# Queries ordered behind products, two fetches on GpSimd, and a third place for the parts of probabilities

## The chip, the core and the metric

The kernel runs on one core of one Trainium2 chip. A core has a matrix engine (TensorE, PE in the profile; PEld is its loading of stationary operands), three engines for elementwise work (VectorE or DVE, ScalarE or ACT, GpSimd or POOL) and a fifth, SyncE (SP), which here only issues transfers. Transfers (DMA) are carried by 16 engines that all issuers share; SP, ACT and POOL each have a queue of their own. Every engine works through its own list of instructions in order and waits, at the head of that list, for semaphores of the others. The metric is the time of one execution on the device in microseconds; several are taken and the median is given.

## The reference

The program is one step of a small hybrid model with two layers, on 256 prompt tokens and 1,024 latent tokens of 1,024 channels, ten tiles of 128 tokens in all.

```python
for l in range(DEPTH):                        # DEPTH = 2
    sh, sc, gt = split_mod(silu(c) @ w_ada[l] + b_ada[l])
    h = rms_norm(x, norm_g[l]) * (1 + sc) + sh
    if l % 2 == 0:                            # gated linear attention, forward and backward scans
        out, state = gla_mixer(h, ...)        # (rms_norm(o_f + o_b) * silu(gate)) @ w_out
    else:                                     # grouped-query softmax attention
        q, k, v, gate = split(h @ w_in)       # 8 query heads, 2 key heads, 128 wide
        q, k = rms_norm(q, qn), rms_norm(k, kn)      # latent tokens: rope_2d as well
        p = softmax(q @ k.T * HEAD_DIM ** -0.5)      # latent: 1024 keys + 256 cached ones
        out = ((p @ v) * silu(gate)) @ w_out
    x = x + gt * out
```

Prompt tokens attend to the 256 prompt keys only. Returned are both groups of tokens, the scan states and the prompt's keys and values.

## The kernel before

To keep the precision of float32, every matrix operand is scaled by a power of two and split into two float16 parts, high and low, and each product is three matmuls: high by high, high by low, low by high (`mm3`, line 124). So most steps have the same form: an engine makes the high part, DVE the low part, and a DMA transpose, issued by SP, turns them so that the contracted index lies on the partitions.

The work has four stages. The first, to about 585 us, is the linear attention: a loop of 50 slots (`gla`, four heads and one more, ten token tiles each), into which a function `filler(slot)` puts other work: weights of later stages, and for the first four latent row tiles the fetch of the branch rows `og_d` with their scaling, splitting and transposing (`out_load`, line 827, and `out_prep`, line 835). The tuple `PREP` names the slots in which this happens, `EARLY` the slots in which the first two of these rows already go through the output product.

The second stage, to about 736 us, is `gla_out` (line 849). It goes over the eight row tiles left, in the order latent, then prompt (`n` is the place in that order, from 2 to 9). At each place it forms the residual tile: the output product `y` on PE, 24 matmuls of 512 columns and 48 of 256, the scaled sum with the input row `xr` (`residual`, lines 810 to 822), the norm and modulation for the next layer (`mod_tile`), and two transposes into `hT_hi` and `hT_lo` (line 377). Between residual tiles it puts key tiles (`key_tile`, 48 matmuls of 256 columns into `kv`, line 1041) and, at the end, the first query tiles (`query`, line 1193, whose matmuls go to `mm`). The branch rows of places 4 and later are fetched here, by `out_load` (line 832), into the two halves of a buffer `og` which lies where the scan's `q` and `k` buffers were; `out_prep` finds their maximum (line 838), makes the high part on ACT (841), the low part on DVE (842), and issues the two transposes on SP (844 and 845). In places 4 and 5 the text calls the tile "row 4" and "row 5".

The third stage, to about 1205 us, is `attention` (line 1205): ten steps `n`, each a pair of a head group and a block of 256 tokens, four heads `e` in each, two query tiles `j` of 128 in each head. For each: the scores `S` on PE (line 1104), the maximum on DVE (1107), the exponential `p` on ACT (1112), then in `rest` (line 1118) the reciprocal of the sum, and the two parts of the probabilities in one buffer `phl`: the high part by POOL where `j` is 0 (1134) and by ACT where it is 1 (1136), the low part by DVE (1137); SP transposes the whole buffer into `PT` (1138), and two heads later PE multiplies `PT` by the values (`values`, line 1151). `phl` has two buffers, used in turn. The keys, values and gates of the prompt and the last key tiles come in the first heads of this stage.

The fourth stage, `att_out`, forms the output product. Its first branch row, 1 MB from `og2_d`, is fetched within the third (`out2_load`, line 1257) into a buffer of the pool `wst`, of which one was given to the transposed queries and the other is free in attention until then. Below, `wst` also names the transposed queries and keys in a row of the profile.

The order of each engine's list is not the order of the Python statements. A planner replays the program with modelled costs and lets each engine take the instruction that it holds to be ready first; `issue_after(x)` keeps all instructions made under it behind instruction `x`. So a matmul whose operands the planner expects early may stand ahead of one that was written before it. Buffers count as well: an instruction may only write a place whose earlier readers are through.

Of the kernel before, what the change touches and what calls it, by code (L numbers as in the profile page):

```python
# [7 lines left out]
F16 = mybir.dt.float16  # L8
BF16 = mybir.dt.bfloat16
F32 = mybir.dt.float32  # L10
# [7 lines left out]
P = 128  # L18
D = 1024
KT = D // P  # L20
TP, TS = 256, 1024
# [3 lines left out]
PAST = 256  # L25
# [11 lines left out]

WO = (30, 32, 36, 38)

PREP = (42, 44, 46, 48)  # L40
EARLY = (45, 47)

AHEAD = (3, 5, 7, 9, 13, 15, 17, 19, 21, 23, 25, 27, 29, 31)
# [10 lines left out]
class K:  # L54
# [69 lines left out]
    def mm3(self, out, lhs, rhs, n=KT):  # L124
        for k in range(n):
            lh, ll = lhs(k)
            rh, rl = rhs(k)
            for j, (a, b) in enumerate(((lh, rh), (lh, rl), (ll, rh))):
                self.nc.tensor.matmul(out, a, b, start=k == 0 and j == 0, stop=k == n - 1 and j == 2)  # L129

    def hT(self, k, a, n):
        return self.hT_hi[:, k, a : a + n], self.hT_lo[:, k, a : a + n]
# [691 lines left out]

    def out_load(self, i, og=None, parts=None):
        if og is None:
            og = self.og[:, i % 2]
            t = self.t(self.xp, [P, 2 * D], F16, "oghl", bufs=2)  # L830
            parts = t[:, 0:D], t[:, D:]
        self.nc.sync.dma_start(og, self.og_d[i])
        return i, og, parts

    def out_prep(self, i, og, parts):
# [13 lines left out]
    def gla_out(self, wo, early, n0):  # L849
        nc = self.nc  # L850
        order = [2, 3, 4, 5, 6, 7, 8, 9, 0, 1]
        prep = dict(zip(order, early))
        self.inv_h = self.mod1[3]
        self.og = self.t(self.xp, [P, 2, D], F32, "og")
        half = self.t(self.xp, [P, 2, KT, 256], F16, "wkv")
        xs, rows = {}, {}

        def load(n):
            if n < NT:
                xs[n] = self.t(self.xp, [P, D], F32, "xr", bufs=4)  # L860
                (nc.gpsimd if n < n0 + 2 else nc.sync).dma_start(xs[n], xrow(self.I, order[n]))

        load(n0)
        load(n0 + 1)
        for n in range(len(early), n0 + 4):
            rows[n] = self.out_load(order[n])
        ckv = self.att_load()
        for n in range(n0, NT):
            i = order[n]
            if n == NT - 1:  # L870
                self.query_rest()
                self.query()
                self.key_tile(order[n - 2], wkv)
                self.query_rest()
            hT, lT, inv = prep.pop(i)
            x = xs.pop(n)
            last = self.residual(i, lambda k: (hT[:, k, :], lT[:, k, :]), wo, inv, x)
            nc.gpsimd.dma_start(self.x1_d[i], x)
            self.last = last
            with self.tc.issue_after(last):  # L880
                if n + 2 in rows:
                    prep[order[n + 2]] = self.out_prep(*rows.pop(n + 2))
            load(n + 2)
            if n + 4 in range(len(early), NT):
                rows[n + 4] = self.out_load(order[n + 4])
            t = self.t(self.xp, [P, 2, D], F16, "hl", bufs=2)
            if i == 0:
                self.rows_load(0)
            self.mod_tile(i, x, (t[:, 0], t[:, 1]), self.last)
            for j in {3: (0,), 4: (1, 2), 5: (3,), 6: (4,), 7: (5,), 8: (6,)}.get(n, ()):  # L890
                self.key_tile(order[j], wkv)
            if n == 8:
                self.query()
            if n == n0:
                d, inv = self.ahead["kv"]
                wkv = []
                for j, (hi, lo) in enumerate((
                    [t[:, :, 256:512] for t in self.nw[0:2]], (half[:, 0], half[:, 1])
                )):
                    b = slice(256 * j, 256 * j + 256)  # L900
                    nc.sync.dma_start(hi, d[:, 0, :, b])
                    nc.sync.dma_start(lo, d[:, 1, :, b])
                    wkv.append((hi, lo, 256))
                with self.tc.issue_after(last):
                    self.att_setup(*ckv)
                    self.key_setup(*ckv, inv)
            if n == 4:
                self.q0 = self.t(self.wp, [P, KT, 512], F16, "whi2")
                nc.sync.dma_start(self.q0, self.ahead["q0"][0][:, 0])
            if n == 7:  # L910
                self.query_start()
        self.query_low()
        return wkv[0]
# [204 lines left out]
    def rest(self, after=None):  # L1118
        if self.put_off is None:
            return  # L1120
        if after is not None:
            with self.tc.issue_after(after):
                return self.rest()
        nc = self.nc
        p, den, PT, j, nk = self.put_off
        self.put_off = None
        r = self.t(self.sm, [P, 1], F32, "srec")
        nc.vector.reciprocal(r, den)  # L1128
        r2 = self.t(self.sm, [P, 1], F32, "srec2")
        nc.vector.tensor_scalar(r2, r, 2.0 ** 14, None, ALU.mult)  # L1130
        parts = self.t(self.sp, [P, 2 * (TS + PAST)], F16, "phl")[:, 0 : 2 * nk]
        hi, lo = parts[:, 0:nk], parts[:, nk:]
        if j == 0:
            nc.gpsimd.tensor_scalar(hi, p, r, 2.0 ** 14, ALU.mult, ALU.mult)  # L1134
        else:
            nc.scalar.activation(hi, p, AF.Copy, scale=r2)  # L1136
        nc.vector.scalar_tensor_tensor(lo, p, r2, hi, ALU.mult, ALU.subtract)  # L1137
        nc.sync.dma_start_transpose(PT[:, 0 : 2 * nk // P, j * P : j * P + P], parts)  # L1138
# [66 lines left out]
    def attention(self, wo, wk):  # L1205
        self.S0, self.put_off = self.t(self.ps, [P, 1536], F32, "S"), None
        wq, wg, q, g = self.wq, self.wg, self.q, {}
        pend, later = [], []
        t = self.t(self.sp, [P, 20, 256], F16, "PT", bufs=3)[:, 0:16, :].rearrange("p (j k) n -> p j k n", j=2)
        for j in range(2):  # L1210
            self.nc.sync.dma_start(t[:, j], self.ahead["kv"][0][:, j, :, 256:512])
        wkv = [wk, (t[:, 0], t[:, 1], 256)]
        for n, (p, c) in enumerate(self.steps):
            if n == 1:
                wq.append(self.load_w("q1", 1, later))
            if n == 4:
                wg.append(self.load_w("g1", (2, 0), later))
            if n == 6:
                wo.append(self.wload("o0", (0, 2), later))
            if n == 9:  # L1220
                wo.append(self.wload("o1", 1, later))
            for e in range(4):
                h = 4 * p + e
                if later:
                    self.nc.sync.dma_start(*later.pop(0))
                PT = self.t(self.sp, [P, 20, 256], F16, "PT", bufs=3)
                self.scores(h, c, 0, q[(p, c, 0)], PT)
                if e % 2 == 0:
                    self.query()
                    self.rest()  # L1230
                    self.scores(h, c, 1, q[(p, c, 1)], PT)
                else:
                    self.query_rest()
                if len(pend) == 2:
                    self.values(*pend[0], g.pop(pend.pop(0)[0]))
                else:
                    self.key_tile(len(pend), wkv)
                if e % 2 == 1:
                    self.scores(h, c, 1, q[(p, c, 1)], PT)
                pend.append((h, c, PT))  # L1240
                if e % 2 == 1:
                    g.update({i: self.gateT(i, c, *wg[p]) for i in (h - 1, h)})
                    self.rest()
                if n == 9 and e == 0:
                    row = self.out2_load(OUT[0])
                if n == 9 and e == 1:
                    first = self.ropet.rearrange("p a b d -> p (a b d)").bitcast(F16)
                    first = first.rearrange("p (j h t) -> p j h t", j=2, h=AH)
                    with self.tc.issue_after(self.last):
                        self.prep = self.out2_prep(row, (first[:, 0], first[:, 1]))  # L1250
        self.fold_gate(*self.gate_load(1), wo[0][2] + wo[1][2])
        wo[:] = [(hi, lo, 512) for hi, lo, _ in wo]
        self.out_tile(OUT[0], 0, self.t(self.sp, [P, TS + PAST], F32, "p")[:, 0:D], wo)
        for t in pend:
            self.values(*t, g.pop(t[0]))
# [50 lines left out]
def emit(ctx, tc, I, O, dbg=None, stop=None):  # L1306
# [29 lines left out]
    with ExitStack() as c:  # L1336
# [102 lines left out]
        def filler(slot):  # L1439
# [32 lines left out]
            if slot == 40:  # L1472
# [7 lines left out]
                k.rows_load(1)  # L1480
            if slot in PREP:
                n = PREP.index(slot)
                a = k.t(k.wst, [P, KT, 256], F32, "wst").rearrange("p k n -> p (k n)")[:, 0:D]
# [138 lines left out]
```

## Time and profile before

| | |
|---|---|
| median of 3 runs (lowest to highest) | 1309.43 us (1306.7 to 1311.03) |
| the profiled execution | 1308.64 us |
| its span, first to last instruction | 1306.6 us |
| busy in the span: PE, DVE, ACT, POOL | 93%, 71%, 54%, 28% |
| mean busy share of the 16 transfer engines, `gla_out` and attention to 1130 us | 0.79 and 0.71 |

All times in rows of the profile count from the start of the span. A row of the list of groups or of the timeline names the line of the kernel, the engine, the operation, the written and the read tile, the shape and how many instructions it merges; a bracket at the end of a timeline row gives the idle time of the engine before it and what ended it. `SPq` is SP's queue: its durations are the times that the issuing took. A row of the list of waits reads: engine, tile and line that waited, for whom, microseconds in total, how often, the longest one. Buffer numbers are left out, so `mm` stands for query products, gates and values alike.

### The profile page before, as it was taken

What the parts mean: (1) busy time and instruction counts of PE and PEld (TensorE: products, weight loads), DVE (VectorE), ACT (ScalarE), POOL (GpSimd) and SP (SyncE); (2) the same over time, 40 slices, a digit from 0 to 9 for tenths busy, and PEclk for the clock granted to TensorE, in tenths of its full rate; (3) what the DMA queues carried; (4) which work ended last, traced back from release to release, by engine and by line L of the source; (5) the groups of instructions that cost most, each with busy time, mean ns of one, the idle gap of its engine ahead of it and who ended that gap; (6) DMA issues with size and microseconds to landing.
All of it is one profiled execution on the core that took longest, in us unless ns stands there. A gap on an engine that the chain in (4) does not pass through costs nothing. (4 is left out here: it accounts for less than half of the span.)

```text
span 1306.6 us, 22246 instructions
## 1 busy us (share of the span) xinstructions
PE 1215.6 (93%) x7936; PEld 783.7 (60%) x7936; DVE 924.6 (71%) x2120; ACT 705.4 (54%) x1706; POOL 360.7 (28%) x594
## 2 busy tenths in 40 slices
PE   3899999999998989796999989999998999989998
PEld 2366666555645556574777557667665767766444
DVE  5575879877876798676776767777767587785652
ACT  3684656565655566541333376766766686673110
POOL 1132214223321143410223334342232345322000
PEclk9899999999998999998999999999999999999999
DMA  9712655554646343269956597666957648879342
GB/s 359 251 33 82 211 158 175 172 162 135 187 135 193 118 145 114 88 159 284 240 129 170 146 209 142 129 138 131 199 108 157 142 95 146 185 140 227 128 150 81
DMA packets 357454, 207.51 MB, mean 159 GB/s; under 512 B 251054, under 2 KB 341438, under 8 KB 354912
## 3 DMA queue, kind: packets, MB, share of 16 engines
q1 hardware_dynamic: 349824, 188.02, 56.2%
q0 software_dynamic: 4080, 12.73, 3.2%
q10 hardware_dynamic: 3440, 5.35, 1.1%
q8 instruction: 62, 1.02, 0.3%
q14 instruction: 48, 0.39, 0.1%
HBM read 107.45 MB, written 37.26 MB: 111 GB/s over the span
## 5 line engine op out<-in xcount | busy, mean ns | idle before, releaser
L129 PEld LDWEIGHTS <-hT_hi 128*128 128x128 f16 x1920 | 188.6, 98 | 133.4 <-issue 18.4
L129 PE MATMUL mm<-whi,hT_hi 128*128 128x512 f16 (+1 forms) x576 | 200.4, 348 | 13.7 <-DMA whi<-w_q 8.9
L129 PE MATMUL mm<-whi,hT_lo 128*128 128x512 f16 (+1 forms) x576 | 200.1, 347 | 0.1
L129 PE MATMUL mm<-wlo,hT_hi 128*128 128x512 f16 (+1 forms) x560 | 194.2, 347 | 0.0
L129 PEld LDWEIGHTS <-whi 128*128 128x128 f16 x1232 | 121.1, 98 | 61.3 <-issue 2.5
L1137 DVE SCALAR_TENSOR_TENSOR phl<-p,srec,phl 128x1280 f16<-128x1280 f32 (+1 forms) x80 | 108.7, 1360 | 68.5 <-POOL phl L1134 35.7
L129 PE MATMUL mm<-hT_hi,whi 128*128 128x256 f16 (+1 forms) x480 | 142.1, 296 | 0.0
L129 PE MATMUL mm<-hT_lo,whi 128*128 128x256 f16 (+1 forms) x480 | 142.0, 296 | 0.0
L129 PE MATMUL mm<-hT_hi,wlo 128*128 128x256 f16 (+1 forms) x480 | 141.9, 296 | 0.0
L129 PEld LDWEIGHTS <-hT_lo 128*128 128x128 f16 x960 | 94.5, 98 | 65.7 <-DMA hT_lo<-k 3.4
L1104 PE MATMUL S<-kT,wst 128*128 128x512 f16 (+1 forms) x624 | 122.0, 338 | 9.9 <-ACT p L1112 8.7
L129 PE MATMUL mm<-PT,vh 128*128 128x256 f16 x672 | 114.0, 275 | 11.8 <-DMA PT<-phl 8.7
L1107 DVE TENSOR_REDUCE smx<-S 128x1 f32<-128x1280 f32 (+1 forms) x80 | 101.6, 1269 | 14.3 <-PE S L1104 14.2
L1134 POOL TENSOR_SCALAR phl<-p,srec 128x1280 f16<-128x1280 f32 (+1 forms) x40 | 56.0, 1401 | 192.6 <-DVE srec L1128 77.7
L1112 ACT ACTIVATE p<-S,snb,sexp 128x1280 f32<-128x1280 f32 (+1 forms) x80 | 99.4, 1242 | 5.6 <-DVE phl L1137 1.8
L1104 PEld LDWEIGHTS <-wst 128*128 128x128 f16 x624 | 60.9, 98 | 62.3 <-issue 10.3
L129 PE MATMUL mm<-PT,vl 128*128 128x256 f16 x336 | 92.6, 276 | 0.0
L152 DVE TENSOR_REDUCE wmx<-wst 128x1 f32<-128x512 f32 x104 | 64.8, 677 | 21.2 <-DMA wst<-in_att_w_in 7.8
L129 PEld LDWEIGHTS <-vh 128*128 128x128 f16 x672 | 65.7, 99 | 23.3 <-issue 9.6
L129 PEld LDWEIGHTS <-wlo 128*128 128x128 f16 x616 | 60.6, 98 | 31.7 <-DVE wlo L1275 1.8
L942 POOL TENSOR_TENSOR rope<-hx,ropet 128x64 f32<-128x64 f32 x160 | 63.2, 425 | 30.7 <-ACT hx L1068 18.2
L1109 ACT ACTIVATE snb<-smx,nsexp 128x1 f32<-128x1 f32 x80 | 23.3, 291 | 74.9 <-DVE smx L1107 72.9
(370 smaller groups left out, 2710.2 us busy)
## 6 DMA issues: line engine op xcount, KB each, us to landing
wada<-in_w_ada SPq DMA_DIRECT2D x16, 1024.0 KB
wst<-in_gla_w_in SPq DMA_DIRECT2D x12, 1024.0 KB
wst<-in_att_w_in SPq DMA_DIRECT2D x10, 1024.0 KB
og_d<-gx SPq DMA_DIRECT2D x40, 128.0 KB
og_d<-og POOLq DMA_DIRECT2D x40, 128.0 KB, 2.8
wst<-og_d SPq DMA_DIRECT2D x5, 1024.0 KB
xr<-x_d SPq DMA_DIRECT2D x9, 512.0 KB
out<-xr ACTq DMA_DIRECT2D x17, 256.0 KB
```

The source lines that it names most:

```text
L129: self.nc.tensor.matmul(out, a, b, start=k == 0 and j == 0, stop=k == n - 1 and j == 2)
L152: nc.vector.tensor_reduce(mx[:, j : j + 1], st[:, 2 * j : 2 * j + 2, :], AX.XY, ALU.max, apply_absolute_value=True)
L942: nc.gpsimd.tensor_tensor(tv[:, h, :, w, :], xv[:, h, :, 1 - w, :], sn[:, :, w, :], ALU.mult)
L1104: nc.tensor.matmul(S[:, a : a + n], x, y, start=m == 0, stop=m == 2)
L1107: last = nc.vector.tensor_reduce(mx, S, AX.X, ALU.max).ins
L1109: nc.scalar.activation(nb, mx, AF.Copy, scale=self.nsexp)
L1112: nc.scalar.activation(p, S, AF.Exp, scale=self.sexp, bias=nb, accum_out=den)
L1134: nc.gpsimd.tensor_scalar(hi, p, r, 2.0 ** 14, ALU.mult, ALU.mult)
L1137: nc.vector.scalar_tensor_tensor(lo, p, r2, hi, ALU.mult, ALU.subtract)
```

## The change

Four edits. (1) `PREP` moves the preparation of the second to fourth row tile to earlier slots. (2) The branch rows of places 4 and 5 are fetched by POOL's queue instead of SP's. (3) `mm3` remembers its last matmul in `self.pe`, and both calls of `query` in `gla_out` are made under `issue_after(self.pe)`, so that all of the query's instructions stay behind the last matmul that was written before. (4) In attention the second `wst` buffer is taken as a third place for the parts of the probabilities: a counter `turn` goes 0, 1, 2, and at 0 the parts go to the third place, at 1 and 2 to the `phl` buffers as before. From step 8, head 3 on, only the `phl` buffers are used.

```diff
-PREP = (42, 44, 46, 48)
+PREP = (42, 43, 45, 46)
...
-                self.nc.tensor.matmul(out, a, b, start=k == 0 and j == 0, stop=k == n - 1 and j == 2)
+                self.pe = self.nc.tensor.matmul(out, a, b, start=k == 0 and j == 0, stop=k == n - 1 and j == 2).ins
...
-    def out_load(self, i, og=None, parts=None):
+    def out_load(self, i, og=None, parts=None, load=None):
...
-        self.nc.sync.dma_start(og, self.og_d[i])
+        (load or self.nc.sync).dma_start(og, self.og_d[i])
...
         for n in range(len(early), n0 + 4):
-            rows[n] = self.out_load(order[n])
+            rows[n] = self.out_load(order[n], load=nc.gpsimd)
...
             if n == NT - 1:
                 self.query_rest()
-                self.query()
+                with self.tc.issue_after(self.pe):
+                    self.query()
...
             if n == 8:
-                self.query()
+                with self.tc.issue_after(self.pe):
+                    self.query()
...
-        parts = self.t(self.sp, [P, 2 * (TS + PAST)], F16, "phl")[:, 0 : 2 * nk]
+        parts = self.t(self.sp, [P, 2 * (TS + PAST)], F16, "phl") if self.turn or self.third is None else self.third
+        parts = parts[:, 0 : 2 * nk]
+        self.turn = (self.turn + 1) % 3
...
+        third = self.t(self.wst, [P, KT, 256], F32, "wst").rearrange("p k n -> p (k n)").bitcast(F16)
+        self.third, self.turn = third[:, 0 : 2 * (TS + PAST)], 0
...
+                if n == 8 and e == 3:
+                    self.third = None
                 if n == 9 and e == 0:
                     row = self.out2_load(OUT[0])
```

## The prediction

> **What bounds the kernel now.** I read the page's first part, then the busy time of each engine in each stretch, and then the list of who made TensorE (PE) wait.
>
> ```profile
> PE 1215.6 (93%) x7936; PEld 783.7 (60%) x7936; DVE 924.6 (71%) x2120; ACT 705.4 (54%) x1706; POOL 360.7 (28%) x594
> 584.00:736.00 152.00, 140.22 (x1018) 100.34 (x1017) 106.27 (x237) 52.04 (x129) 40.97 (x79) 0.96 0.79 196
> 736.00:1130.00 394.00, 377.86 (x2684) 262.60 (x2682) 281.58 (x560) 269.64 (x672) 138.90 (x215) 1.00 0.71 146
> 1130.00:1225.00 95.00, 85.61 (x575) 56.41 (x574) 66.17 (x113) 43.20 (x78) 20.27 (x30) 0.98 0.77 180
> ```
>
> In the last three rows the first number behind the window is its length, then busy PE, weight loads, DVE, ACT and POOL. PE is busy 93% of the span. The change has only PE's gaps to win: 11.8 us in `gla_out` (584 to 736), 16.1 us in most of attention (736 to 1130), 9.4 us in its end. Who makes PE wait from 584 to 640 (from 625 to 740 the list is empty):
>
> ```profile
> PE mm L129 <- DMA whi<-w_q: 8.9, 1, 8.9
> PE y L129 <- DMA hT_lo<-k: 2.9, 1, 2.9
> ```
>
> The first three of the list from 740 to 1130, and the same wait as the second in the list from 736 to 1225:
>
> ```profile
> PE S L1104 <- ACT p L1112: 5.5, 3, 3.0
> PE mm L129 <- DMA PT<-phl: 4.2, 3, 1.8
> PE mm L129 <- ACT snb L1109: 3.1, 2, 2.1
> ```
>
> ```profile
> PE mm L129 <- DMA PT<-phl: 8.7, 6, 2.0
> ```
>
> So one wait of 8.9 us for the query weights, and 4.2 us (8.7 with the end) for transposed probabilities, are what the parts of the change aim at.
>
> **PREP (42, 43, 45, 46).** The order of instructions of each engine is the same in both kernels up to the first residual tiles: the engines' planner had those rows where they are already. I cost it at nothing. The 2.9 us wait on `hT_lo<-k`, which is such a row, stays.
>
> **Queries behind products.** Here is PE around the query wait.
>
> ```profile
> 619.44 1.01 PE L129 MATMUL mm<-whi,hT_hi 128*128 128x512 f16 x2 [8.90 <-DMA whi<-w_q]
> 620.35 0.41 PE L129 MATMUL kv<-whi,hT_hi 128*128 128x256 f16 x1
> 623.43 0.27 PE L129 MATMUL kv<-whi,hT_hi 128*128 128x256 f16 x1
> 627.21 0.38 PE L129 MATMUL y<-whi,hT_hi 128*128 128x512 f16 x1
> 627.42 0.38 PE L129 MATMUL y<-wlo,hT_hi 128*128 128x512 f16 x1
> 637.63 0.27 PE L129 MATMUL kv<-whi,hT_hi 128*128 128x256 f16 x1
> ```
>
> Before, two query matmuls stand at the head of PE's queue, wait for their weights, and behind them a key tile (kv) runs 620.35 to 627.21, then the residual tile (y) of row 4, 10.42 us, to 637.63. In the changed order both query matmuls have gone to the other queries later, and y of row 4 comes first, then the key tile. But row 4 is not there at 619.4. The engines ahead of it:
>
> ```profile
> 598.68 0.10 PEld L129 LDWEIGHTS <-hT_lo 128*128 128x128 f16 x1 [3.36 <-DMA hT_lo<-k]
> 604.86 0.92 SPq L832 DMA_DIRECT2D og<-og_d  x2
> 612.69 5.62 SPq L844 DMA_TRANSPOSE hT_hi<-oghl  x1
> 618.40 4.39 SPq L845 DMA_TRANSPOSE hT_lo<-oghl  x1
> 609.35 1.22 DVE L838 TENSOR_REDUCE wm<-og 128x1 f32<-128x1024 f32 x1 [6.69 <-DMA og<-og_d]
> ```
>
> SP issues row 4's two transposes behind the query weights, from 612.69 to 622.79. They make packets under 512 bytes, so the DMA view shows when they move; below are its counts from 622.0 to 624.4 and from 624.4 to 626.
>
> ```profile
> DMA packets 2189, 0.71 MB, mean 295 GB/s; under 512 B 2144, under 2 KB 2144, under 8 KB 2189
> DMA packets 213, 0.47 MB, mean 292 GB/s; under 512 B 105, under 2 KB 105, under 8 KB 213
> ```
>
> Row 4's lower half lands at about T = 624.2. Before, the key tile hid this (y began at 627.21). Now y meets it. After T come y (10.42 us), and what stood from 619.44 to 627.21 without the two query matmuls (7.77 - 2 x 0.21 = 7.35): the first 3.8 us or so of that run slow after the idle time (0.42 us for a kv matmul at 620.35, 0.27 at 623.43), which the restart costs again. Four y matmuls (4 x 0.21 = 0.84) need only the upper half and go while PE waits; the two query matmuls (0.42) are paid later. The next key tile starts at T + 10.42 + 7.35 - 0.84 against 637.63, and 0.42 is owed: the cost is T - 620.3. At T = 624.2 that is +3.9 us. The list of waits is empty up to 740, so nothing behind it takes this up.
>
> **Two branch fetches on GpSimd.** They decide T. SP saves the 0.92 us of issue in the row of 604.86; POOL spends an issue for each fetch instead, and issues its own next things, the stores of rows, behind them; its long idle times here (40.97 us busy of 152) hide that, and without them it would cost about the same 0.92. The destination is free only when the transpose shown at 598.68 has landed, so the fetch leaves at about 598.7 instead of 604.86, and DVE's wait of 6.69 us ends earlier. But the transposes stand behind the same SP queue. What the transfer engines had left (busy tenths, 598 to 604 at 0.15 us a digit, then 604 to 612 at 0.2):
>
> ```profile
> DMA  9989999999999999999999999000000008999999
> DMA  8996999911120599998987997798799779988999
> ```
>
> There are 8 empty digits near 602 (1.2 us) and five low ones near 606 (1.0 us): if the megabyte fills them, all that follows on the SP queue comes up to 2.2 us earlier, plus nothing where the data aren't there. T is thus 621.8 to 624.2, the cost +1.5 to +3.9. I take T = 623.0, about half of the slack: **+2.7**. The Trainium skill (DMA: Bandwidth & Descriptors, "Issuing engines are not separate DMA queues") says that transfers from any issuing engine interleave on the same 16 engines, and that spreading them saves only issue time. By that rule alone T would be 624.2 - 0.92 = 623.3 and the cost +3.0; the empty digits say that a little more may come.
>
> **The third place.** Parts of probabilities rotate over three places instead of two; the third is an unused weight buffer. Who waits for a place, 740 to 1130, and one case that reaches PE:
>
> ```profile
> POOL phl L1134 <- DMA PT<-phl: 36.5, 6, 8.2
> ACT phl L1136 <- DMA PT<-phl: 7.1, 6, 2.3
> ```
>
> ```profile
> 1002.82 2.25 POOL L1134 TENSOR_SCALAR phl<-p,srec 128x1280 f16<-128x1280 f32 x1 [7.15 <-DMA PT<-phl]
> 1009.12 0.38 PE L129 MATMUL mm<-PT,vh 128*128 128x256 f16 x2 [1.75 <-DMA PT<-phl]
> ```
>
> POOL and ACT lose 43.6 us to full places, but PE feels only the 4.2 us in three waits. With the place free 5 to 7 us sooner those three go. What is late next is DVE: the 3.1 us on `snb` end behind its maximum, and stay. Ends: 0 (each wait replaced by one on DVE) and -7.3 (both kinds go). I take -3.5, most of the 4.2. The 8.7 of the last row isn't reached: the third place is given up in step 8, at head 3.
>
> **What the third place moves.** First, ACT's order near 770. In the changed order the key copy `hx` (the row of 771.58), which waits for POOL's store, stands ahead of a `phl` part and of the exponential that PE waits for:
>
> ```profile
> 771.58 0.47 ACT L1047 ACTIVATE hx<-mm,inv_k 128x256 f32<-128x256 f32 x1 [3.08 <-DMA out<-hx]
> 772.91 1.42 ACT L1112 ACTIVATE p<-S,snb,sexp 128x1280 f32<-128x1280 f32 x1
> 774.30 1.36 ACT L1136 ACTIVATE phl<-p,srec 128x1280 f16<-128x1280 f32 x1
> 776.92 0.46 ACT L1055 ACTIVATE rope<-mm,inv_av 128x256 f32<-128x256 f32 x1
> 774.47 1.78 PE L1104 MATMUL S<-kT,wst 128*128 128x512 f16 x9 [2.24 <-ACT p L1112]
> 777.44 0.38 PE L129 MATMUL mm<-whi,hT_hi 128*128 128x512 f16 x1 [1.19 <-ACT rope L1055]
> ```
>
> The exponential starts 1.33 us after `hx` now. After, 1.36 for the `phl` part and about 1.5 for seven small operations come between: PE's scores start near 777.3, 2.8 late. They take 1.78 us, and the next product, which waited till 777.44, starts at 779.1: **+1.6** net; ends 0 (if that store lands sooner) and 2.8. Second, the load of the first branch row for the last product (1 MB) now shares the buffer with the third place; SP issues it behind the last transpose from there:
>
> ```profile
> 1141.37 11.37 SPq L1138 DMA_TRANSPOSE PT<-phl  x3
> 1156.08 6.42 DMA PT<-phl
> ```
>
> SP must wait until that transpose, issued at 1141.37, has landed, some 6 us by the second row (of the chain), so the next one, near 1146, goes about 1.7 us later, and the megabyte moves beside them. The place is near the chain that ends last. Ends 0 and +2; I take **+0.5**.
>
> **Sum.** +2.7 - 3.5 + 1.6 + 0.5 = +1.3 us on the profiled execution's 1308.64 us: 1309.9, said as 1310.0. That execution lies 0.8 us below the median of 1309.43. A difference of 0.3% (3.9 us) is about what a measurement of this kernel can tell from no change.
>
> **Rivals.**
> A, slower: the third place relieves engines for which nobody waits. DVE's parts and maxima (281.58 us of 394) stay in one queue, PE's three waits turn into waits on DVE, and the late exponential costs all of its 2.8 us: 1308.64 + 2.7 + 0 + 2.8 + 0.5 = 1314.6. For it: the 43.6 us against 4.2. It decides where the third place gains less than about 2 us. Against it: POOL's 7.15 us before 1002.82 ends just ahead of PE's 1.75.
> B, faster: with POOL's and ACT's parts sooner, DVE's queue moves up as well, and both the 4.2 and the 3.1 us go, with T = 621.8 and no cost at the end: 1308.64 + 1.5 - 7.3 + 1.6 = 1304.4; 1300.6 if the 3.8 us of score waits behind 1130 went too. Against it: the waits on `snb` follow DVE work that waited for no place.
> C: the rows are truly sooner and land at 619.4, so that y starts where the query did: T - 620.3 = -0.9 and a total of 1306.3. It needs 4.8 us where I see 2.2.
> D: the change doesn't do what it says. It renames the query wait, the places were never short where it counts, and the planner's order costs as little: within a microsecond of 1309.
>
> **Numbers.** The forecast (within 3 us of 1310) has 0.42, A 0.28, B 0.20, C 0.05, D 0.05. Within 0.3%: most of the forecast, C and D, 0.47. Slower: A and the forecast's upper edge, 0.31. Faster: B with a little, 0.22. The range runs from between B's two ends, 1303, to 1317 (A with T = 624.2 and the load's +2 is 1317.3).
>
> **What would show it.** In the changed profile: no wait on `w_q` near 619, but one of 11 to 14 us by y on `hT_hi<-oghl` or `hT_lo<-oghl`, ending at 621.8 to 624.2; the first kv of the second key tile at 639 to 641.5; the 2.9 us at 598 as before; POOL's waits on `PT<-phl` far below 36.5 us, PE's below 1; the scores near 774 later by 2 to 3 us against their surroundings; the load of the first branch row near 1147 instead of before. I am wrong if T is far from 623, if PE's total of waits from 740 to 1130 moves by more than 5 us, or if a wait appears between 625 and 740.

## The result, and the profile after

The changed kernel is slower: 1318.0 us (1314.19 to 1321.45, 5 runs) against 1309.43, a ratio of 1.0086 with a 95% interval of 1.0065 to 1.0107. This ratio, like all below, is taken from fast runs alone (one of the kernel before took 4446.23 us); the quotient of the two medians is 1.0065. Run once more beside the experiments the changed kernel gave 1.0056 (1.0037 to 1.0075). The forecast was 1310.0 with a range of 1303 to 1317; the time lies just above it.

The page's first part, then PE's waits from 584 to 640 and from 985 to 1132 us:

```profile
span 1316.4 us, 22275 instructions
PE 1217.9 (93%) x7936; PEld 785.1 (60%) x7936; DVE 927.1 (70%) x2120; ACT 706.2 (54%) x1706; POOL 368.3 (28%) x596
```

```profile
PE y L129 <- DMA hT_hi<-oghl: 15.0, 1, 15.0
PE y L129 <- DMA hT_lo<-k: 1.7, 1, 1.7
```

```profile
PE S L1106 <- ACT p L1114: 4.1, 2, 2.2
PE mm L129 <- DMA PT<-phl: 3.4, 2, 2.6
```

Before, the list of that last stretch read:

```profile
PE mm L129 <- DMA PT<-phl: 3.0, 2, 1.8
PE S L1104 <- ACT p L1112: 0.3, 1, 0.3
```

The 9 us wait on query weights is gone and a wait of 15.0 us on row 4 stands there. And the waits of the scores on the exponential, 0.3 us before, are 4.1 us now.

Where the time went is read by counting along PE's list of 7,936 matmuls, which holds the same work in nearly the same order in all these kernels, and comparing the start of the matmul with the same number. Each column of the table is one stretch, from the matmul of the column before to its own; it says by how many us the stretch took longer than in the profile of before. The kernels besides the changed one are those of the next section.

| up to matmul (start before) | 3,330 (591) | 4,250 (729) | 4,500 (769) | 6,000 (988) | 7,000 (1132) | 7,500 (1210) | last |
|---|---|---|---|---|---|---|---|
| changed | -2.9 | +3.3 | +1.7 | -6.3 | +7.0 | +2.8 | +4.1 |
| changed, again | -5.3 | +3.5 | +1.5 | -6.5 | +8.4 | +1.8 | +0.4 |
| PREP only | -2.8 | +3.9 | -0.3 | -2.3 | -0.1 | -1.7 | +0.4 |
| without third place | -2.2 | +6.5 | +1.4 | -1.5 | -0.5 | -1.4 | +0.1 |
| queries only | -2.0 | -2.1 | +1.2 | -3.6 | -0.1 | -1.3 | +0.2 |
| fetches only | +0.4 | +2.9 | -0.1 | -1.4 | -0.3 | -0.3 | +0.8 |
| queries, fetches, key tile first | +0.5 | -4.4 | +0.2 | -1.6 | -0.2 | -0.5 | -0.1 |
| third place only | -3.5 | -0.6 | 0.0 | -5.7 | +8.5 | +1.0 | -0.2 |
| third place to step 5 | +0.2 | +1.9 | -0.1 | -6.0 | -0.1 | -0.6 | +0.8 |
| third place from step 5 | +1.0 | +1.8 | +0.2 | -0.7 | +6.7 | -0.4 | +0.9 |
| third place, maxima first | +3.6 | -1.4 | -0.3 | -5.2 | -0.3 | +3.3 | -0.3 |
| the same, to step 7 | -5.4 | +4.5 | +0.1 | -5.3 | +1.3 | -0.4 | 0.0 |
| two places, maxima first | -5.6 | +2.4 | +0.3 | -1.0 | +4.1 | -1.1 | +1.9 |

In the first column all kernels do the same, so it shows chance: 9 us from lowest to highest. The second column shows chance too: kernels whose second stage is that of before have -1.4 to +4.5 there, PREP alone +3.9. Much of it is the wait on `hT_lo<-k`, from none to 6.0 us in these profiles. It drops out where one counts from the matmul that ends this wait, number 3,369 (598.7 us before), to number 3,700, behind the second key tile (654.9). There the kernels with the order of before take -0.7 to +2.8 us longer than the profile of before; the four in which row 4 comes first (the changed one twice, the one without the third place, the fetches alone) take 4.1 to 4.4; the queries alone take -3.3, and the one with the key tile first -1.5. From 6,000 to 7,000 chance is small: the profiles without a third place differ by 0.5 us there, the reordered maxima aside. From 4,500 to 6,000 they took 0.7 to 3.6 us less than the profile of before, which was slow there by chance (PREP alone, the same program, has -2.3); a third place's gain counts from those.

### The profile page after: what moved, and what is told of

Read it like the earlier page. It is cut to its first block, busy times and chain, and to the rows that moved or that the text cites. A ratio compares the mean times of both kernels' runs of the same rounds, so it can differ in the third digit from the quotient of the medians.

```text
span 1316.4 us, 22275 instructions
## 1 busy us (share of the span) xinstructions
PE 1217.9 (93%) x7936; PEld 785.1 (60%) x7936; DVE 927.1 (70%) x2120; ACT 706.2 (54%) x1706; POOL 368.3 (28%) x596
## 5 line engine op out<-in xcount | busy, mean ns | idle before, releaser
L129 PE MATMUL mm<-PT,vh 128*128 128x256 f16 x672 | 116.9, 279 | 10.7 <-DMA PT<-phl 10.7
L1141 DVE SCALAR_TENSOR_TENSOR phl<-p,srec,phl 128x1280 f16<-128x1280 f32 (+1 forms) x56 | 77.4, 1384 | 36.9 <-POOL phl L1138 20.9
L1138 POOL TENSOR_SCALAR phl<-p,srec 128x1280 f16<-128x1280 f32 (+1 forms) x28 | 39.6, 1414 | 122.9 <-DVE srec L1130 89.5
L120 POOL TENSOR_TENSOR hrs<-hrsa,mhalf 128x2 f32<-128x2 f32 x50 | 40.7, 816 | 78.7 <-DVE hrsa L118 78.5
```

The lines of the kernel that those rows point to most:

```text
L120: nc.gpsimd.tensor_tensor(r, a, self.mhalf[:, 0:w], ALU.pow)
L129: self.pe = self.nc.tensor.matmul(out, a, b, start=k == 0 and j == 0, stop=k == n - 1 and j == 2).ins
```

## The experiments

Each ratio is to the kernel before, run beside it on the same chip.

**PREP alone.**

```diff
-PREP = (42, 44, 46, 48)
+PREP = (42, 43, 45, 46)
```

> Only PREP is changed. The order of every engine's instructions is the same as before. If that is all that counts: ratio 1.000, within 2 us of before, and its profile shows by how much identical programs differ from run to run (in the scan part up to 585 us, and in the loads of the last stage). The rival, that the earlier call still frees or fills a buffer at another time: faster by the 2.9 us by which the changed kernel was ahead at 580 us.

Measured: 0.9995 (0.9968 to 1.0023). It is the same program in another text: PE's and SP's lists are the same, instruction for instruction. So its profile shows how far chance alone goes: the wait on `hT_lo<-k`, which this tuple was meant to touch, is 2 us longer.

**Without the third place: edits 1 to 3.** The diff is the shown one without its part on `rest` and `attention`.

> PREP, the two fetches on GpSimd and the ordered queries, without the third place. If the parts add up as the changed profile shows (the second stage gives +3.1 us, the rest stems from the third place): +3 us, ratio 1.0024, row 4's tile of y starting near 620 to 623, the last stage as before. The rival, that the slow load at 1250 us in the changed kernel comes from the second stage's order or from chance: +3 without it, up to +7 with it.

Measured: 1.0022 (0.9997 to 1.0048), 2.9 us, which agrees with the sum of this part but is not clear of zero. The slow branch load at 1250 us isn't there (+0.1 in the last stretch). The column up to matmul 4,500, where ACT's order was to cost 1.6 us, was a surprise: +1.4 us without a third place. And row 4's tile starts at 624.2, later than the 620 to 623 expected.

**Queries alone, and fetches alone.** One with edit 3, the other with edit 2 alone.

> Only the queries are ordered behind the products. If, against what I wrote, not this edit but the two fetches put the residual tile of row 4 ahead of the key tile: the key tile starts at once near 610.5 instead of waiting behind the query matmuls, y then waits for row 4 until about 624 instead of starting at 627.2 and restarts slow (1.9 us), so -1 us, ratio 0.999. The rival, that this edit alone makes the swap, as in the prediction: +3, ratio 1.002.

> Only the two fetches go to GpSimd; both query matmuls keep their place ahead. If the fetches make the swap: PE waits for the query weights as before (9 us) and then again for row 4 until 621.8 to 624.2, the key tile behind both; +2 to +4 us, ratio 1.002 to 1.003. The rival, that the fetches only bring the row sooner: 0 to -2.

Measured: queries 0.9978 (0.9955 to 1.0001), fetches 1.0039 (1.0020 to 1.0058). The interval of the queries just reaches 1, that of the fetches is clear of it. So my reading of the edits was crossed. PE's waits from 584 to 640 with the queries alone (two rows), and with the fetches alone:

```profile
PE kv L87 <- DVE amx L1001: 5.8, 1, 5.8
PE y L129 <- DMA hT_lo<-k: 3.8, 1, 3.8
```

```profile
PE mm L129 <- DMA whi<-w_q: 11.3, 1, 11.3
PE y L129 <- DMA hT_hi<-oghl: 2.8, 1, 2.8
PE y L129 <- DMA hT_lo<-k: 1.5, 1, 1.5
```

With the queries alone the key tile keeps its place ahead of row 4's residual tile and only waits for DVE's key scales (5.8 us in place of 8.9). With the fetches alone, the two query matmuls wait as before and the first 24 matmuls of the residual tile, now ahead of the key tile, wait again; the other 48 follow the key tile. It is the fetches that make the swap. Since the planner places by the readiness that it expects, it must hold row 4 to be ready sooner than it is.

**Queries and fetches, with the key tile kept first.** This undoes the swap and leaves the fetches on GpSimd.

```diff
                 self.key_tile(order[j], wkv)
+                self.pe_kv = self.pe
...
+            with ExitStack() as c:
+                if n == 4:
+                    c.enter_context(self.tc.issue_after(self.pe_kv))
-            last = self.residual(i, lambda k: (hT[:, k, :], lT[:, k, :]), wo, inv, x)
+                last = self.residual(i, lambda k: (hT[:, k, :], lT[:, k, :]), wo, inv, x)
```

> Ordered queries and the two fetches on GpSimd, with the residual tile of row 4 held behind the key tile. If the loss of the second stage is the swap of these two tiles and not the fetches: like the ordered queries alone or better, since row 4 lands 1 to 2 us sooner, -3 to -5 us, ratio 0.997. The rival, that the fetches on GpSimd cost by themselves: +2 to +4, ratio 1.002 to 1.003, as with the fetches alone.

Measured: 0.9971 (0.9949 to 0.9993). PE's list is now, matmul for matmul, that of the queries alone. The fetches cost nothing by themselves that these runs can tell; the order that they led to does. Whether they gain anything beside the ordered queries (0.9978) can't be told either.

**The third place alone, and only a part of its time.** Edit 4 alone; the same with `if n == 5 and e == 0` for giving it up; the same from `n == 5` on.

> Only the third place. If it costs what the changed profile shows behind 736 us (key copies on ACT +1.6, attention up to 1130 us +0.6 to +1, its end +2.8, and the branch load at 1250 us +4.1): +9 us, 1318.5, ratio 1.007. The rival, that the load at 1250 us was chance: +5, 1314.5, ratio 1.004. What I had forecast for this part: -1.4.

> The third place is given up at step 5 instead of in step 8, so that the load of the first branch row can go out long before the end. If the place itself gains while it is there (the changed kernel had won 6 us at 988 us against 850 us) and the loss lies in its late part and the late load: ACT's +1.6 and -3 to -6, that is 1305 to 1308, ratio 0.997 to 0.999. The rival, that the third place's order costs as much as it gains in every stretch: 1310 to 1312, ratio 1.001 to 1.002.

> The third place only in steps 5 to 8. If the stretches add up (steps 0 to 4 alone were measured at -5, the whole at +2.7): +7 to +8 us, ratio 1.006, with PE's waits near 1004 and 1084 us as with the whole. The rival, that the loss needs both halves (a rotation that is out of step with the heads): at most +3.

Measured: alone 1.0021 (0.9993 to 1.0050), given up at step 5 0.9962 (0.9936 to 0.9987), from step 5 on 1.0049 (1.0024 to 1.0075). The stretches add up: in steps 0 to 4 the place gains 5 us, in steps 5 to 8 it loses 6 to 7. The 9 us that I expected of the whole had taken the load at 1250 us for a part of it; that load took 8.85 us in the changed kernel's first profile and 5.67 in that of before (rows of the two chains). PE waits 2.3 us behind it in the first (first row below, of the list from 1240 on), and at most 1.0 us in every other profile, that of the changed kernel run again included:

```profile
PE mm L87 <- DVE wm L1280: 2.3, 1, 2.3
```

```profile
1250.18 8.85 DMA wst<-og_d
```

```profile
1244.97 5.67 DMA wst<-og_d
```

**Why steps 5 to 8 lose: the order of scores, maxima and low parts.** This is the changed kernel, POOL, DVE and PE ahead of the wait near 1004, and then DVE at the same place before:

```profile
996.62 1.59 POOL L1138 TENSOR_SCALAR phl<-p,srec 128x1280 f16<-128x1280 f32 x1 [5.20 <-DVE srec L1130]
998.24 3.01 DVE L1141 SCALAR_TENSOR_TENSOR phl<-p,srec,phl 128x1280 f16<-128x1280 f32 x2 [1.15 <-POOL phl L1138]
1001.17 1.48 DVE L1109 TENSOR_REDUCE smx<-S 128x1 f32<-128x1280 f32 x1
1004.63 0.59 PE L1106 MATMUL S<-kT,wst 128*128 128x512 f16 x2 [1.82 <-ACT p L1114]
1009.00 0.28 PE L129 MATMUL mm<-PT,vh 128*128 128x256 f16 x1 [2.58 <-DMA PT<-phl]
```

```profile
1002.32 1.55 DVE L1137 SCALAR_TENSOR_TENSOR phl<-p,srec,phl 128x1280 f16<-128x1280 f32 x1 [0.83 <-ACT phl L1136]
1005.10 1.55 DVE L1137 SCALAR_TENSOR_TENSOR phl<-p,srec,phl 128x1280 f16<-128x1280 f32 x1 [1.24 <-POOL phl L1134]
1006.57 1.48 DVE L1107 TENSOR_REDUCE smx<-S 128x1 f32<-128x1280 f32 x1
```

Two low parts (998.24, 3.01 us) stand ahead of the maximum at 1001.17 on DVE; DVE waits 1.15 us for POOL's high part with the maximum behind it, and PE's next scores wait for the exponential of that maximum. But before, DVE has the same order here. What is new near 1004 is PE's order: before, the product of `PT` and the values (1009.12, shown in the prediction) comes ahead of the next scores, and in the changed kernel the scores come first and wait. PE falls 4.4 us back between matmuls 6,128 and 6,217 and wins 1.4 back by 6,300. Near 1084 it is DVE's order that is new, the changed kernel first and then before:

```profile
1078.04 1.55 DVE L1141 SCALAR_TENSOR_TENSOR wst<-p,srec,wst 128x1280 f16<-128x1280 f32 x1 [1.15 <-POOL wst L1138]
1079.51 1.61 DVE L1141 SCALAR_TENSOR_TENSOR phl<-p,srec,phl 128x1280 f16<-128x1280 f32 x1
1081.04 1.48 DVE L1109 TENSOR_REDUCE smx<-S 128x1 f32<-128x1280 f32 x1
1084.49 3.26 PE L1106 MATMUL S<-kT,wst 128*128 128x512 f16 x9 [2.24 <-ACT p L1114]
```

```profile
1079.07 1.55 DVE L1137 SCALAR_TENSOR_TENSOR phl<-p,srec,phl 128x1280 f16<-128x1280 f32 x1 [0.83 <-ACT phl L1136]
1080.54 1.48 DVE L1107 TENSOR_REDUCE smx<-S 128x1 f32<-128x1280 f32 x1
1082.04 1.69 DVE L1137 SCALAR_TENSOR_TENSOR phl<-p,srec,phl 128x1280 f16<-128x1280 f32 x1
```

Here a second low part has moved ahead of the maximum, and PE falls back by another 4.3 us between matmuls 6,600 and 6,760. The experiment has the parts of a head's first query tile written behind the maximum of its second from step 5 on, once with the third place and once with two places:

```diff
                 if e % 2 == 0:
                     self.query()
-                    self.rest()
+                    if n < 5:
+                        self.rest()
```

> The third place as in the changed kernel, but from step 5 on the parts of a head's first query tile are written behind the maximum of its second, so that DVE's low part, which waits for POOL, can't stand ahead of that maximum. If this order on DVE causes the late exponentials near 1004 and 1084 us: those waits go, 4 to 6 us less than with the third place alone, 1303 to 1305, ratio 0.997 to 0.999. The rival, that full queues of transposes cause them: as the third place alone, +2.7, ratio 1.002.

> Two places, as before, with the maxima ahead from step 5 on. If the order on DVE was a loss only beside a third place: 0 to +2 us, ratio 1.000 to 1.0015. The rival, that this order gains by itself and hid the third place's loss where both were tried: -3 us, ratio 0.998.

Measured: with the third place 0.9997 (0.9976 to 1.0019), with two places 1.0029 (1.0009 to 1.0050). Both are slower than expected: the first gains 3 us on the third place alone instead of 4 to 6, the second loses 3.8 instead of at most 2. PE's waits from 985 to 1132 us, first with the third place alone, then with the maxima first, then with two places and the maxima first:

```profile
PE S L1104 <- ACT p L1112: 4.1, 2, 2.3
PE mm L129 <- DMA PT<-phl: 3.7, 2, 2.4
```

```profile
PE mm L129 <- DMA PT<-phl: 1.9, 2, 1.5
PE mm L129 <- ACT phl L1138: 0.8, 1, 0.8
PE S L1104 <- ACT p L1112: 0.4, 1, 0.4
```

```profile
PE S L1104 <- ACT p L1112: 4.4, 3, 2.2
PE mm L129 <- DMA PT<-phl: 3.2, 2, 1.7
```

The same edit takes the 4.1 us of score waits away beside a third place (to 0.4) and brings 4.4 us beside two, where they were 0.3. So the place and the edit each cost time here without the other, and none together: what counts is the order that the planner makes of them. The stretch to matmul 7,000 goes from +8.5 to -0.3 us. That the scores wait for late maxima is shown by both places and by this run; what of the gain is the maximum and what the rest of the order on PE and DVE, which moved too, wasn't separated.

**The late load.** What that kernel still loses is +3.3 us from matmul 7,000 to 7,500. The same with the place given up at `n == 7 and e == 0`:

> The third place with the maxima ahead from step 5 on, as before, and given up at step 7, so that the load of the first branch row goes out near 1060 us, 14 transposes earlier. If that run's loss from 1132 to 1179 us (about 4 us) comes from the late load and SP's wait for its buffer: 3 to 4 us faster than it, -4 us against before, ratio 0.997. The rival, that the end of attention pays for the earlier gain whatever is loaded there: as that run, 0, ratio 1.000.

Measured: 0.9972 (0.9955 to 0.9989). SP's queue in the changed kernel (two rows), in this one (last row):

```profile
1140.52 3.72 SPq L1142 DMA_TRANSPOSE PT<-wst  x1
1147.56 0.32 SPq L1268 DMA_DIRECT2D wst<-og_d  x1
```

```profile
1048.63 0.32 SPq L1266 DMA_DIRECT2D wst<-og_d  x1
```

In the changed kernel SP stands until 1147.56 for a transpose that it issued at 1140.52, and sends 1 MB ahead of the next. With the load at 1048.63 the stretch takes -0.4 us. PE's longest wait for `PT` from 1132 to 1200 was 4.5 us in the changed kernel, 5.5 in the one with the maxima first, and is 2.0 here and before. Giving the place up early also changes steps 7 and 8 (+1.3 in the stretch before) and PE's order from matmul 7,347 on, so the 3.7 us between these two runs aren't the load's alone. What belongs to the load is seen better across all profiles. The five of kernels that send it late lose 4.3 to 5.6 us between matmuls 7,100 and 7,200, after gaining 1.1 to 2.2 in the hundred matmuls before; none of the other profiles loses more than 0.9 there.

**The changed kernel again, and the parts that gain.** The first is the changed kernel. The other three combine ordered queries with: the third place to step 5; the maxima first and the place to step 7; the fetches with the key tile first and the place to step 5.

> The changed kernel once more, beside the others. If its parts add up (ordered queries with the fetches +2.9 us, third place +2.7): +5.6 us, ratio 1.004, and the last stage without the 2.5 us wait near 1262 us that its first profile had. The rival, that the parts make each other worse: +11, ratio 1.0086, as it was first measured, with that wait again.

> The two edits that gain by themselves: ordered queries (-2.9 us) and the third place given up at step 5 (-5). If they add up: -8 us, ratio 0.994. The rival, that the late key copies on ACT near 770 us, which come with the ordered queries, take what the third place gives there: -4 to -5, ratio 0.9965.

> The same with the queries ordered behind the products. If all of it adds up: -7 us, ratio 0.995. The rival as for the ordered queries with the place given up at step 5: -3 to -4, ratio 0.997.

> Ordered queries, the fetches with the key tile ahead, and the third place given up at step 5. If all add up: -8 to -10 us, ratio 0.992 to 0.994. The rival, that the fetches give nothing beside the ordered queries: as without them, ratio 0.993.

Measured: the changed kernel 1.0056 (1.0037 to 1.0075), without the wait near 1262. Ordered queries and the place to step 5: 0.9927 (0.9903 to 0.9950), medians of 1299.08 us against 1307.43. The other two 0.9938 (0.9913 to 0.9964) and 0.9952 (0.9928 to 0.9976); the last fell short of the 0.992 to 0.994 expected, and gives no sign that the fetches help. So the parts add up, within the intervals, in the slow and in the fast direction, and three versions beat both kernels; which of the three is best isn't settled.

## Why the prediction was wrong, step by step

**PREP, 0.** Right: 0.9995.

**Second stage, +2.7.** Near in size, but put to the wrong edit. The table's +3.3 and +3.5 can't show the size, since PREP alone has +3.9. Counted from matmul 3,369 it is 4.1 to 4.4 us against the profile of before, a little over the upper end of 3.9, and some 3.5 against the mean of all kernels with that order (+0.8). Here is PE at row 4 and at the second key tile in the changed kernel:

```profile
619.79 0.61 PE L129 MATMUL y<-whi,hT_hi 128*128 128x512 f16 x1 [14.96 <-DMA hT_hi<-oghl]
637.66 0.27 PE L129 MATMUL kv<-whi,hT_hi 128*128 128x256 f16 x1
```

This profile was 2.9 us ahead of before at matmul 3,330, which puts y at 622.6 in the time of before and the key tile at 640.5; at matmul 3,369 it was 4.0 us ahead, which puts them at 623.8 and 641.7. The second count is the one to trust: it puts y at 623.8 to 624.2 in all four profiles with this order, the first at 622.6 to 626.4. So T = 623.0 was a little early, and what y met was close to the 624.2 of before. Three details were off. Only y's first 24 matmuls stand ahead of the key tile, the other 48 behind it. y waited for the upper half of row 4, not the lower, so the four early matmuls had nothing to fill. And the wait is 15.0 us instead of 11 to 14, since PE came there sooner. But the step "In the changed order both query matmuls have gone to the other queries later, and y of row 4 comes first" ran two edits together: with the queries ordered alone the key tile stays ahead and the ratio is 0.9978, and only the fetches, which I had let bring the row sooner, put y first. SP's transposes of row 4 in the changed kernel:

```profile
608.63 6.71 SPq L844 DMA_TRANSPOSE hT_hi<-oghl  x1
615.43 3.18 SPq L845 DMA_TRANSPOSE hT_lo<-oghl  x1
```

They end at 618.61, 4.2 us earlier than before (622.79) in a profile that was already 4.0 us ahead. From matmul 3,369 to that end it is 23.9 to 25.0 us in the six profiles with the fetches on GpSimd, and 23.0 to 26.3 in the eleven with the fetches on SP. So the slack of 2.2 us that I saw in the transfer engines brought nothing that these profiles show, nor can they show the 0.92 us of issue: behind the other work of SP's queue the transposes come when they came before. The Trainium skill (DMA: Bandwidth & Descriptors, "Issuing engines are not separate DMA queues") says that another issuing engine saves only the time of issuing; these 23.9 to 25.0 against 23.0 to 26.3 us agree in that no saving beyond it is seen.

**The third place, -3.5.** This step failed. With the third place alone the two stretches from 4,500 to 7,000 take +2.8 us, in the changed kernel +0.6 and +1.9. The early steps gained what I took for the whole: -5.2 to -6.5 in the table, some 4 against programs without the place. From 860 to 992 us PE waits for nothing in the changed kernel. Before, it had waited 4.3 us there (3.5 in PREP alone), the 3.1 us on `snb` among them, as rival B had it:

```profile
PE mm L129 <- ACT snb L1109: 3.1, 2, 2.1
PE mm L129 <- DMA PT<-phl: 1.2, 1, 1.2
```

But the later steps lost 6.7 to 8.5 (column 7,000). The failing sentence was "What is late next is DVE: the 3.1 us on `snb` end behind its maximum, and stay." I let the queues keep their order and only priced the waits that a free place ends. In its place the runs showed a new order: scores ahead of the values on PE near 1004 and low parts ahead of the maximum on DVE near 1084, which brought 4.1 us of score waits where there had been 0.3. Rival A named DVE, but as a limit on the gain, not as a loss. The places' waits did go, as said: POOL's 36.5 us on `PT<-phl` from 740 to 1130 are no longer in the list. POOL waits for DVE instead, the row below and 51.1 us more with the third place (`wst`), against 70.4 us before:

```profile
POOL phl L1138 <- DVE srec L1130: 89.5, 18, 8.5
```

**ACT's order near 770, +1.6.** Right in size (+1.7 and +1.5), and again put to the wrong edit: with the third place alone the stretch takes 0.0, without it +1.4. ACT's list has the order foretold only in the changed kernel and in the one without the third place, so it comes with the ordered queries and the fetches together. The queries alone, and with the key tile first, keep ACT's order of before (the +1.2 of the queries alone isn't explained by it). In the changed kernel the scores wait there like this:

```profile
774.04 1.34 ACT L1140 ACTIVATE wst<-p,srec 128x1280 f16<-128x1280 f32 x1
775.29 1.40 ACT L1114 ACTIVATE p<-S,snb,sexp 128x1280 f32<-128x1280 f32 x1
776.84 2.81 PE L1106 MATMUL S<-kT,wst 128*128 128x512 f16 x9 [2.42 <-ACT p L1114]
```

The part and the exponential stand in the order foretold, 1.34 us ahead of what PE waits for.

**The late load, +0.5.** Too small: the stretch takes +2.8 and +1.8 us in the changed kernel, +1.0 with the third place alone and -0.4 with it from step 5, and -1.7 to -0.3 in the kernels that send the load earlier. I had SP's next transpose 1.7 us late and let almost nothing follow from it, while PE's wait for `PT` grew from 2.0 to 4.5 us.

**Sum.** Put with what the stretches measured, +3.4, +1.6, +1.3 (for the third place, both profiles' mean) and +2.3 make +8.6 us, between the two ratios (1.0056 and 1.0086 of 1309 us are 7.3 and 11.3). That fits better than it should: chance in the +3.4 alone is some 3 us. What the sum leaves of the first profile's distance is the +4.1 of the last stretch, with the slow load at 1250 us, and the -2.9 of the scan. Of the miss of 7.3 us against the sum forecast, 4.8 lie in the third place and 1.8 in the late load.

## What to carry to other kernels

Where a planner writes the order of each queue, a buffer more or a load elsewhere is an edit of the order of all engines: look for what moved ahead of a wait, in the in-order queue that the bottleneck listens to and in the bottleneck's own, before counting the waits that go away. Cost each edit by its own order, not the whole diff's; two terms here came out near in size and belonged to another edit, and the parts that gained (ordered queries, the place for the early steps) made a kernel 0.7% faster than the one before.

## What the runs showed that I had not expected

Programs with the same order in the scan differed by up to 9 us at matmul 3,330 between profiles, while one stretch of attention (matmuls 6,000 to 7,000) repeats within half a microsecond; how far a single profile can judge has to be found for each stretch. And one 1 MB load took 5.67 and 8.85 us at the same place of two programs in which PE's order near it was the same. The last stretch took 4.1 us longer with the slow load, and 0.4 us in the second profile of the same program.
